# VectorE in place of GpSimd for the low parts of the weights, in the mixers and behind two norms

## The chip, the cores and the metric

The kernel runs on one NeuronCore of a Trainium2 chip. The metric is the device time of one execution in microseconds, from the chip's own clock. The engines are TensorE (PE in the profile; its weight loads are a row of their own, PEld), VectorE (DVE), ScalarE (ACT), GpSimd (POOL) and SyncE (SP), whose queue issues the loads of weights from memory. Each engine works through its own instructions in their order; semaphores order the engines among each other.

## The reference, cut to what matters

Two blocks of a language model follow each other on 256 tokens of width 1024: a first with two layers (a gated delta net and an mLSTM, each followed by a convolutional feed-forward), and a second with one layer (SwiGLU, a stage of three mixers, SwiGLU). Everything is float32. The stage that the change touches most is the mixer stage of the second block:

```python
def second_block(x, mem, ...):
    x = x + 0.5 * swiglu(rmsnorm(x, ffn1_norm), ffn1_w_gu, ffn1_w_down)
    h = rmsnorm(x, mix_norm)
    z = h @ w_in                                    # 1024 x 5280
    u = gelu(z[..., COL_U:COL_V]); v = gelu(z[..., COL_V:COL_CQ])
    y_a = spatial_gating(u, v, sg_ln_g, sg_ln_b, sg_w, sg_b)
    y_b = mla(z[..., COL_CQ:COL_CKV], z[..., COL_CKV:COL_KR], z[..., COL_KR:COL_QM], positions, ...)
    y_c = memory_attention(z[..., COL_QM:COL_GATE], mem, ...)
    gates = sigmoid(z[..., COL_GATE:] + b_gate)     # three gates of width 1024
    merged = (gates[0] * (y_a @ w_branch_a) + gates[1] * (y_b @ w_branch_b) + gates[2] * (y_c @ w_branch_c))
    x = x + merged @ w_out
    x = x + 0.5 * swiglu(rmsnorm(x, ffn2_norm), ffn2_w_gu, ffn2_w_down)

def first_block(x, ...):                            # for each of its two layers
    hs = hs + keep * rms_norm(mix, norm_w[i, 1])    # the sandwich norms: one behind the mixer,
    f = conv_ffn(rms_norm(hs, norm_w[i, 2]), ...)   # one ahead of the feed-forward
    hs = hs + keep * rms_norm(f, norm_w[i, 3])
```

## The kernel before

Activations stand with features on the partitions and tokens along the free axis, so a linear layer is a row of 128x128 weight blocks against 256 to 272 tokens. Float32 products are made of three matmuls: each operand is split into a rounded high part and a low part (what the rounding left), and TensorE adds high times high, high times low and low times high. For weights, `wload` does this block by block: SyncE loads a block of 512 KB into `wraw`, ScalarE rounds it into `wh`, and an elementwise subtraction `wl = wraw - wh` makes the low part. Three buffers of each name rotate (`p_raw` and `p_hl`, three each): a load may start when the subtraction and the rounding have read the old `wraw`, and a rounding may write `wh` when TensorE has read the old one.

Who subtracts is settled in `wload`. On VectorE it is one instruction for the whole block (128x1024); on GpSimd it is two of half the width (128x512). Blocks are counted in `nload`; `seg` counts the stages: 0 the gated delta net, 1 the first feed-forward, 2 the mLSTM, 3 the second feed-forward, 4 the first SwiGLU, 5 the mixers with their output projection, 6 the last SwiGLU. GpSimd subtracts in the delta net and the mLSTM (`ordered` is off there), everywhere in the mixers (`mixing` is on), for the first blocks after a norm in stages 1 and 3 (up to `near_load`, set from `POOL_FIRST`), and for every second or fourth block where `POOL_EVERY` says so.

Behind a sandwich norm (`mix_end`) VectorE works through a chain that is written out by hand: the residual (`mw`, `hst`), the normalized features (`xn`), ScalarE's rounding of them (`xhl`, high) and VectorE's low part of them (`xhl`, low), two of eight features at a time. TensorE starts the next linear layer feature by feature as these arrive (`linears_g`). Then come the feed-forward's evictions `fy`.

In the mixers many short chains run on VectorE beside the big products: the reciprocal square root by Newton steps (`rq_v`, `rq_a`, `rq_y`, a few columns wide), the layer norm of `v` (`sgst`, `sgv`), the rotary embedding of queries and keys (`qtok`, `ktok`, `qsq`), softmax maxima (`smx`), and the eviction `py` of a product in PSUM, whose bank TensorE needs for a later product. The order of TensorE's instructions is settled while the program is built, by a small planner (`Threads`) that keeps a clock per engine and picks the thread whose inputs are due first; it knows the work that goes through `self.V`, `self.A` and `self.G`, but not what goes straight to `nc.gpsimd`. VectorE's and ScalarE's orders come from the framework's scheduler, which has a timeline of its own.

In the profile nearly all instructions have one line, L190 (the recording helper), so groups go by tile names; subtractions sent straight to `nc.gpsimd` have line L383.

Of the kernel before, what the change touches and what calls it, by code (L numbers as in the profile page):

```python
# [78 lines left out]


NW = (0, 1, 1)
POOL_FIRST = (0, 4, 2, 2, 0, 0, 0)
POOL_EVERY = (0, 0, 0, 2, 4, 0, 4)


# [123 lines left out]
class Kern:  # L209
# [147 lines left out]
    def wload(self, w, k0, nk, c0, nc_, pieces=1, late=None, own=None, eng=None):  # L357

        key = w.tensor.name, k0, c0
        if key in self.ready:  # L360
            return self.ready.pop(key)
        tile = own or (lambda name, dt: (self.p_raw if name == "wraw" else self.p_hl).tile(
            [128, nk, nc_], dt, tag=name, name=name))
        r = tile("wraw", F32)
        self.A.ahead = self.V.ahead = self.G.ahead = True
        h, l = tile("wh", F32R), tile("wl", F32R)
        self.SY.dma_start(
            r[:], w[k0 * 128:(k0 + nk) * 128, c0:c0 + nc_].rearrange("(k p) c -> p k c", p=128))
        self.nload = getattr(self, "nload", 0) + 1
        every = POOL_EVERY[self.seg]  # L370
        if eng is not None:
            pass
        elif not self.ordered or self.mixing or self.nload <= self.near_load or every and self.nload % every == 0:
            eng, pieces = self.nc.gpsimd if self.ordered or self.mixing else self.G, 2
        else:
            eng = self.V
        sub = [(slice(k, k + nk // pieces), slice(None)) for k in range(0, nk, nk // pieces)] if nk >= pieces else [
            (slice(None), slice(c, c + nc_ // pieces)) for c in range(0, nc_, nc_ // pieces)]
        inst = self.A.copy(h[:], r[:])

        def low():
            for a, b in sub:
                eng.tensor_tensor(l[:, a, b], r[:, a, b], h[:, a, b].bitcast(F32), ALU.subtract)  # L383

        if late is None:
            low()
        else:
            if self.ordered:
                self.order(inst)
            late.append(low)  # L390
        self.A.ahead = self.V.ahead = self.G.ahead = False
        return h, l
# [315 lines left out]
    def mix_end(self, src, wcol, N, loads=(), late=1, full=True):  # L708


        late = len(loads) - late
        self.prefetch(loads[:late])
        yield self.part_done
        pm = yield from self.colsum_end(0, self.macc[1])
        pb = yield from self.colsum(self.mwacc, N, "pc1")
        yield ["pc0"]
        pa = yield from self.colsum(self.mcross, N, "pc0")
        r = self.sm(N, "rstd", "rstd")
        X = self.xslots(N)
        c = self.ssq[:, T - N:]  # L720
        r2 = self.r = self.sm(N, "rstd2", "rstd2")
        u = self.sm(N, "sqn", "y")
        w = [self.mw[k // 2][:, k % 2:k % 2 + 1, :N] for k in range(2)] + [self.mw[n][:, :, :N] for n in (1, 2, 3)]
        s2 = [self.hst[:, k:k + n, T - N:] for k, n in ((0, 1), (1, 1), (2, 2), (4, 2), (6, 2))]
        y = {}

        def residual(n):
            self.tt(w[n], w[n], r[:, None, :].to_broadcast([128, w[n].shape[1], N]), ALU.mult)
            self.tt(s2[n], s2[n], w[n], ALU.add)

        def high(*ks):
            for k in ks:
                if full:
                    y[k] = self.sm(N, "xn", "y")
                    self.stt(y[k][:], src[k], self.pv(wcol + k), r2[:], ALU.mult, ALU.mult)
                    self.A.copy(X[k][0], y[k][:])
                else:
                    self.act(X[k][0], src[k], AF.Copy, scale=self.pv(wcol + k))

        def low(*ks):  # L740
            for k in ks:
                if full:
                    self.tt(X[k][1], y[k][:], X[k][0].bitcast(F32), ALU.subtract)
                else:
                    self.last_low = self.stt(X[k][1], src[k], self.pv(wcol + k), X[k][0].bitcast(F32), ALU.mult, ALU.subtract)

        def sums():
            self.tt(u[:], pb[:], r[:], ALU.mult)
            self.stt(u[:], pa[:], 2.0, u[:], ALU.mult, ALU.add)
            self.tt(u[:], u[:], r[:], ALU.mult)  # L750
            self.tt(c, u[:], c, ALU.add)

        def token_scale():

            sums()
            self.rstd(r2[:], c, D, NW[1])
            self.near_load = self.nload + POOL_FIRST[self.seg]

        wlow = []
        with self.tc.manual_schedule(engines={mybir.EngineType.DVE, mybir.EngineType.Activation}):  # L760
            self.rstd(r[:], pm[:], D, NW[0])
            self.seg += 1
            self.near_load = 0
            if full:
                sums()
                self.rstd(r2[:], c, D, NW[1], (lambda: residual(0), lambda: residual(1)))
                high(0, 1)
                residual(2)
                low(0, 1)
                high(2, 3)  # L770
                self.prefetch(loads[late:], wlow, self.V)
                residual(3)
                low(2, 3)
                high(4, 5)
                for f in wlow:
                    f()
                residual(4)
                low(4, 5)
                high(6, 7)
                low(6, 7)  # L780
                self.near_load = self.nload + POOL_FIRST[self.seg]
            else:
                residual(0)
                high(0)
                residual(1)
                high(1)
                low(0)
                residual(2)
                high(2, 3)
                low(1)  # L790
                self.prefetch(loads[late:], wlow, self.V)
                residual(3)
                high(4, 5)
                low(2, 3)
                for f in wlow:
                    f()
                residual(4)
                high(6, 7)
                low(4, 5, 6, 7)
                self.mid = token_scale  # L800
        return X
# [1019 lines left out]
    def add_tile(self, m, ps, scale):  # L1821


        if m == 5:
            self.table("natural_log_exp_and_others")
        x = self.x2[m]
        if scale == 0.5:
            y = self.sm(S, "ady", "y")
            self.stt(y[:], ps, scale, self.r[:], ALU.mult, ALU.mult)
            self.tt(x, x, y[:], ALU.add)  # L1830
        else:
            self.stt(x, ps, scale, x, ALU.mult, ALU.add)
        h, l = self.nextX[m]
        w = self.pv(self.nextw + m)
        self.act(h, x, AF.Copy, scale=w)
        self.stt(l, x, w, h.bitcast(F32), ALU.mult, ALU.subtract)
        self.square(self.macc, m, x, S, "ma")
        if m == KD - 2:
            self.th.add([self.early([self.macc], S)])
        elif m == KD - 1:  # L1840
            self.scale_done = Event()
            self.seg += 1
            self.near_load = self.nload + POOL_FIRST[self.seg]
            self.th.add([self.token_scale(self.macc, S, self.scale_done)])

    def mem_prep(self):
# [604 lines left out]
```

## Time and profile before

| what | value |
|---|---|
| median of 3 runs | 1661.56 us (1658.22 to 1662.08) |
| the profiled execution | 1655.78 us, its span 1654.0 us |
| PE busy | 1547.4 us (94%) |
| DVE busy | 1124.6 us (68%) |
| ACT busy | 929.0 us (56%) |
| POOL busy | 581.0 us (35%) |

The profiled execution is one more run, 5.8 us under the median of the three. The span runs from its first to its last instruction; 1.8 us lie around it. A busy row counts the time in which the engine had an instruction in work, also where that instruction was held up. The granted clock is the share of full speed (1 is 2.4 GHz, 0.5 is 1.2 GHz) that TensorE had.

### The profile page before, as it was taken

How to read it: one execution, taken by the hardware profiler on the slowest of the kernel's cores; microseconds unless marked ns; L12 is line 12 of the kernel's file. 1: busy time of each engine (PE TensorE's matmuls, PEld its weight loads, DVE VectorE, ACT ScalarE, POOL GpSimd, SP SyncE). 2: the span in 40 equal slices, each digit the busy share in tenths (PEclk: the TensorE clock that was granted, in tenths of full speed). 3: DMA queues.
4: the chain of work that ended last, by engine and by line, in shares of the span. 5: the costliest groups of instructions: out<-in, count | busy, mean ns of one | idle time of the engine just before them, and what ended most of it. 6: DMA issues, size and time to landing. Idle time of an engine off the chain costs nothing.

```text
span 1654.0 us, 31168 instructions
## 1 busy us (share of the span) xinstructions
PE 1547.4 (94%) x11932; PEld 1461.7 (88%) x11932; DVE 1124.6 (68%) x2231; ACT 929.0 (56%) x1885; POOL 581.0 (35%) x535
## 2 busy tenths in 40 slices
PE   7889888899899999899899999999997899999999
PEld 5778777789799998888799999999986899999987
DVE  6788877757888857357877758665659653566643
ACT  4567667656566645445566645554554664564442
POOL 3674555320200000551143533312265548511221
PEclk9899999999999999999999999999998999999999
DMA  5331221226365553344356665665553435656664
GB/s 160 91 90 52 77 60 45 77 90 196 108 186 187 178 176 112 105 116 133 110 179 190 187 182 156 206 193 176 174 166 106 128 90 156 182 160 192 183 187 153
DMA packets 239099, 235.39 MB, mean 142 GB/s; under 512 B 11510, under 2 KB 226406, under 8 KB 238950
## 3 DMA queue, kind: packets, MB, share of 16 engines
q1 hardware_dynamic: 238326, 231.86, 46.7%
q8 instruction: 94, 1.54, 0.4%
q0 software_dynamic: 496, 1.41, 0.4%
q14 instruction: 55, 0.45, 0.1%
q10 hardware_dynamic: 128, 0.13, 0.0%
HBM read 232.32 MB, written 1.05 MB: 141 GB/s over the span
## 4 chain that ended last, share of the span: by engine, by line
PE 68%; DVE 22%; ACT 5%; DMA 3%; issue 2%; POOL 0%; SPq 0%; ACTq 0%; DVEq 0%; POOLq 0%
PE ps L190 53%; PE pst L190 4%; DVE cy L190 3%; DVE rq_a L190 3%; DVE RT L190 2%; ACT wh L190 2%; DVE wl L190 1%; DVE rq_y L190 1%; DVE xn L190 1%; PE rsp L190 1%; DVE xhl L190 1%; DMA wraw<-in_ffn_w_up_dram 1%; DVE on L190 1%; PE w L190 1%; PE up L190 1%
## 5 line engine op out<-in xcount | busy, mean ns | idle before, releaser
L190 PE MATMUL ps<-xhl,wh 128*128 128x256 f32 (+2 forms) x4496 | 859.6, 293 | 28.2 <-DVE py L190 7.4
L190 PEld LDWEIGHTS ps<-xhl,wh 128*128 128x128 f32 x4496 | 701.4, 192 | 37.9 <-DVE xhl L190 8.0
L190 ACT CAST wh<-wraw 128x1024 fp32r<-128x1024 f32 (+2 forms) x436 | 448.1, 1029 | 382.0 <-PE ps L190 255.7
L190 PE MATMUL ps<-xhl,wl 128*128 128x256 f32 (+2 forms) x2248 | 625.5, 287 | 0.0
L383 POOL TENSOR_TENSOR wl<-wraw,wh 128x512 fp32r<-128x512 f32 (+3 forms) x264 | 336.1, 1297 | 645.1 <-ACT wh L190 597.2
L190 PEld LDWEIGHTS ps<-xhl,wl 128*128 128x128 f32 x2248 | 423.6, 192 | 0.0
L190 DVE TENSOR_TENSOR wl<-wraw,wh 128x1024 fp32r<-128x1024 f32 (+2 forms) x237 | 285.7, 1206 | 166.1 <-ACT wh L190 161.5
L190 POOL TENSOR_TENSOR wl<-wraw,wh 128x512 fp32r<-128x512 f32 x134 | 174.5, 1324 | 150.9 <-ACT wh L190 134.1
L190 PE MATMUL ps<-hh,wh 128*128 128x256 f32 (+1 forms) x1056 | 191.1, 283 | 0.0
L190 PEld LDWEIGHTS ps<-hh,wh 128*128 128x128 f32 x1056 | 163.2, 189 | 0.0
L190 PE MATMUL ps<-hh,wl 128*128 128x256 f32 (+1 forms) x528 | 149.8, 284 | 0.0
L190 DVE SCALAR_TENSOR_TENSOR fy<-ps,pvt,fy 128x256 f32<-128x256 f32 (+2 forms) x176 | 84.9, 488 | 25.7 <-ACT fy L190 23.8
L190 PEld LDWEIGHTS ps<-hh,wl 128*128 128x128 f32 x528 | 99.4, 188 | 0.2 <-DVE wl L190 0.2
L190 DVE SCALAR_TENSOR_TENSOR cy<-cx,pvt,cy 128x271 f32<-128x271 f32 (+2 forms) x96 | 74.4, 778 | 13.7 <-ACT cy L190 12.7
L190 DVE TENSOR_TENSOR hh<-fy,hh 128x256 fp32r<-128x256 f32 (+1 forms) x88 | 66.3, 755 | 14.0 <-ACT hh L190 13.9
L190 POOL MEMSET mvt<- 128x4 f32 x4 | 0.4, 102 | 176.1 <-PE ps L190 176.1
L190 DVE TENSOR_TENSOR py<-ps,rstd 128x256 f32<-128x256 f32 x72 | 30.1, 421 | 38.0 <-PE ps L190 38.0
L190 ACT ACTIVATE fy<-ps,pvt 128x272 f32<-128x272 f32 (+1 forms) x88 | 49.6, 568 | 10.8 <-PE ps L190 10.2
L190 PE MATMUL pst<-wh,hh 128*128 128x512 f32 x176 | 55.1, 394 | 0.0
L190 ACT CAST hh<-fy 128x256 fp32r<-128x256 f32 (+1 forms) x88 | 35.7, 407 | 29.0 <-DVE fy L190 28.4
L190 PE MATMUL ps<-og,wh 128*128 128x272 f32 x256 | 49.5, 291 | 0.1
L190 DVE CAST_PREDICATED RT<-lvl,w 128x512 f16<-128x512 uint8 x67 | 44.9, 684 | 6.7 <-PE w L190 6.3
(521 smaller groups left out, 2400.6 us busy)
## 6 DMA issues: line engine op xcount, KB each, us to landing
wraw<-in_ffn_w_up_dram SPq DMA_DIRECT2D x88, 512.0 KB
wraw<-in_ffn_w_gu_dram SPq DMA_DIRECT2D x88, 512.0 KB
wraw<-in_ffn_w_down_dram SPq DMA_DIRECT2D x79, 512.0 KB
wraw<-in_gdn_w_in_dram SPq DMA_DIRECT2D x48, 512.0 KB
wraw<-in_w_in_dram SPq DMA_DIRECT2D x41, 512.0 KB
wraw<-in_ml_w_in_dram SPq DMA_DIRECT2D x24, 512.0 KB
wraw<-in_gdn_w_out_dram SPq DMA_DIRECT2D x16, 512.0 KB
wraw<-in_mem_w_kv_dram SPq DMA_DIRECT2D x8, 512.0 KB
```

The costliest lines, as they stand in the source:

```text
L190: r = f(*args, **kw)
L383: eng.tensor_tensor(l[:, a, b], r[:, a, b], h[:, a, b].bitcast(F32), ALU.subtract)
```

## The change

VectorE makes all low parts of weights in the mixers (stage 5). Behind the sandwich norms a table `QUIET` says for how many blocks GpSimd stays out, in place of a table that says for how many it is put in: three blocks in stages 1 and 3 (in stage 1 GpSimd has no later turn either). In stage 3 GpSimd's turn at every second block begins after these three. All else in `wload` stays.

```diff
-POOL_FIRST = (0, 4, 2, 2, 0, 0, 0)
+QUIET = (0, 3, 0, 3, 0, 0, 0)
 POOL_EVERY = (0, 0, 0, 2, 4, 0, 4)
...
         if eng is not None:
             pass
-        elif not self.ordered or self.mixing or self.nload <= self.near_load or every and self.nload % every == 0:
-            eng, pieces = self.nc.gpsimd if self.ordered or self.mixing else self.G, 2
+        elif not self.ordered or self.nload > self.near_load and every and self.nload % every == 0:
+            eng, pieces = self.nc.gpsimd if self.ordered else self.G, 2
         else:
             eng = self.V
...
-                self.near_load = self.nload + POOL_FIRST[self.seg]
+                self.near_load = self.nload + QUIET[self.seg]
```

GpSimd's list loses 8 half subtractions in the first feed-forward, 6 in the second and 120 in the mixers (110 of them 128x512, the rest of smaller blocks): 4, 3 and 60 blocks. VectorE gains as many whole subtractions. SyncE's list is the same.

On VectorE, behind the first norm (stage 1), the four blocks come in between the last two pairs of features and among the evictions of the feed-forward:

```order
 L190 TENSOR_TENSOR hst<-hst,mw 128x544
 L190 TENSOR_TENSOR xhl<-xn,xhl 128x272 x2
+L190 TENSOR_TENSOR wl<-wraw,wh 128x1024
 L190 SCALAR_TENSOR_TENSOR xn<-hst,pvt,rstd_6112 128x272 x2
+L190 TENSOR_TENSOR wl<-wraw,wh 128x1024
 L190 TENSOR_TENSOR xhl<-xn,xhl 128x272 x2
 L190 SCALAR_TENSOR_TENSOR fy<-ps,pvt,fy 128x271 x2
 L190 SCALAR_TENSOR_TENSOR fy<-ps,pvt,fy 128x270 x2
+L190 TENSOR_TENSOR wl<-wraw,wh 128x1024
```

Two subtractions now stand inside the chain of the features, one ahead of `xn` and one ahead of the last `xhl`; behind the norm of stage 3 it is the same pattern.

On VectorE in the mixers, from the middle of the two layer norms (`sgv` is scaled by `sglg`, then shifted by `sglb`) to the evictions `py` of the first products of `u`:

```order
+L190 TENSOR_TENSOR wl<-wraw,wh 128x1024
 L190 TENSOR_TENSOR sgv<-sgv,sglg 128x512
-L190 SCALAR_TENSOR_TENSOR rq_a<-rq_y 128x4
-L190 SCALAR_TENSOR_TENSOR rq_y<-rq_a,rq_y 128x4
+L190 TENSOR_TENSOR py<-ps,rstd 128x256
+L190 SCALAR_TENSOR_TENSOR rq_a<-rq_y 128x4
+L190 SCALAR_TENSOR_TENSOR rq_a<-rq_y 128x1
+L190 SCALAR_TENSOR_TENSOR rq_y<-rq_a,rq_y 128x4
+L190 TENSOR_TENSOR py<-ps,rstd 128x256
 L190 TENSOR_TENSOR sgv<-sgv,sglb 128x512
```

The subtraction shown is the fifth since the first `sgst`; the first `py` stands ahead of the three wide operations of the second layer norm, behind which it stood before. Four more subtractions follow up to the first finished `qtok`.

On TensorE at the same place, between the products of `u` (`ps`, the last two rows of them) and the transposes of the queries (`qktp`):

```order
 L190 MATMUL ps<-xhl,wh 128x256 x2
 L190 MATMUL ps<-xhl,wl 128x256
+L190 MATMUL pst<-wh,xhl 128x512 x2
+L190 MATMUL pst<-wl,xhl 128x512
+L190 MATMUL pst<-wh,xhl 128x512 x2
+L190 MATMUL pst<-wl,xhl 128x512
...
 L190 MATMUL qktp<-eye,qtok 96x128 x4
```

Six such groups of three matmuls (the projection of the memory queries) are moved from behind the transposes to ahead of them.

## Rows read from the trace of the kernel before

**Rows 1.** The page's costliest groups: name, count, busy us, mean ns, idle before.

```profile
L383 POOL TENSOR_TENSOR wl<-wraw,wh 128x512 fp32r<-128x512 f32 (+3 forms) x264 | 336.1, 1297 | 645.1 <-ACT wh L190 597.2
L190 DVE TENSOR_TENSOR wl<-wraw,wh 128x1024 fp32r<-128x1024 f32 (+2 forms) x237 | 285.7, 1206 | 166.1 <-ACT wh L190 161.5
```

**Rows 2.** Timeline of VectorE behind the first norm: start us, us, what.

```profile
435.69 0.79 DVE L190 TENSOR_TENSOR xhl<-xn,xhl 128x272 fp32r<-128x272 f32 x2
436.39 0.91 DVE L190 SCALAR_TENSOR_TENSOR xn<-hst,pvt,rstd 128x272 f32<-128x272 f32 x2
...
439.75 2.94 DVE L190 TENSOR_TENSOR xhl<-xn,xhl 128x272 fp32r<-128x272 f32 x2
442.61 2.93 DVE L190 SCALAR_TENSOR_TENSOR xn<-hst,pvt,rstd 128x272 f32<-128x272 f32 x2
445.47 1.01 DVE L190 TENSOR_TENSOR xhl<-xn,xhl 128x272 fp32r<-128x272 f32 x2
```

**Rows 3.** Timeline of GpSimd, behind the first norm and in the mixers.

```profile
439.51 5.74 POOL L383 TENSOR_TENSOR wl<-wraw,wh 128x512 fp32r<-128x512 f32 x4 [82.24 <-ACT wh L190]
...
1239.26 12.52 POOL L383 TENSOR_TENSOR wl<-wraw,wh 128x512 fp32r<-128x512 f32 x10 [2.18 <-ACT wh L190]
```

**Rows 4.** Windows: us, busy of PE, PEld, DVE, ACT, POOL (instructions), clock, DMA share, GB/s.

```profile
439.00:449.00 10.00, 6.57 (x28) 5.57 (x28) 7.69 (x9) 3.15 (x7) 5.74 (x4) 0.66 0.51 157
815.00:825.00 10.00, 7.22 (x34) 6.42 (x35) 7.80 (x10) 3.30 (x7) 5.32 (x5) 0.66 0.51 151
...
1237.88:1257.58 19.70, 13.38 (x92) 12.61 (x90) 19.49 (x46) 8.85 (x14) 12.52 (x10) 0.91 0.60 174
1250.00:1276.00 26.00, 16.36 (x95) 13.28 (x94) 25.97 (x93) 7.71 (x15) 10.15 (x9) 0.80 0.35 101
1300.00:1350.00 50.00, 43.09 (x327) 40.05 (x327) 39.58 (x138) 28.75 (x74) 23.03 (x18) 0.97 0.37 110
...
1360.00:1400.00 40.00, 40.00 (x339) 39.71 (x339) 15.72 (x37) 20.43 (x34) 30.13 (x24) 1.00 0.52 147
```

**Rows 5.** Groups of VectorE from 1239.35 to 1251.8 us, columns as in rows 1.

```profile
L190 DVE TENSOR_TENSOR rq_a<-rq_a,rq_v 128x1 f32<-128x1 f32 x4 | 5.0, 1257 | 0.0
L190 DVE SCALAR_TENSOR_TENSOR rq_y<-rq_a,rq_y 128x1 f32<-128x1 f32 x4 | 3.8, 974 | 0.0
L190 DVE SCALAR_TENSOR_TENSOR rq_a<-rq_y 128x1 f32<-128x1 f32 x4 | 3.3, 857 | 0.0
```

**Rows 6.** Timeline of VectorE in the mixers, from the first layer norm to `py`.

```profile
1237.88 0.70 DVE L190 BATCH_NORM_STATS2 sgst<-sgv 128x6 f32<-128x512 f32 x1 [1.34 <-ACT sgv L190]
...
1239.20 0.16 DVE L190 SCALAR_TENSOR_TENSOR rq_a<-rq_y 128x1 f32<-128x1 f32 x1
...
1257.58 0.42 DVE L190 TENSOR_TENSOR py<-ps,rstd 128x256 f32<-128x256 f32 x1
```

**Rows 7.** Timeline of TensorE: the two longest waits in the mixers, in brackets.

```profile
1258.06 0.80 PE L190 MATMUL ps<-xhl,wh 128*128 128x256 f32 x2 [6.79 <-DVE py L190]
...
1266.37 0.64 PE L190 MATMUL qktp<-eye,qtok 128*96 128x128 f32 x4 [2.52 <-DVE qtok L190]
```

**Rows 8.** Groups of VectorE from 1257.6 to 1266.3 us, ahead of the first transposes.

```profile
L190 DVE TENSOR_TENSOR qsq<-qtok,rcos 128x64 f32<-128x64 f32 x3 | 1.7, 576 | 0.0
L190 DVE SCALAR_TENSOR_TENSOR rq_y<-rq_a,rq_y 128x4 f32<-128x4 f32 x4 | 1.7, 430 | 0.0
L190 DVE TENSOR_TENSOR qsq<-qtok,rsin 128x64 f32<-128x64 f32 x2 | 1.5, 753 | 0.0
```

**Rows 9.** Groups of VectorE from 1300 to 1338.2 us, the three costliest of 25.

```profile
L190 DVE TENSOR_TENSOR rq_a<-rq_a,rq_v 128x4 f32<-128x4 f32 x15 | 4.3, 299 | 0.1
L190 DVE SCALAR_TENSOR_TENSOR rq_a<-rq_y 128x4 f32<-128x4 f32 x15 | 4.3, 293 | 0.1
L190 DVE SCALAR_TENSOR_TENSOR rq_y<-rq_a,rq_y 128x4 f32<-128x4 f32 x15 | 3.8, 261 | 0.1
```

**Rows 10.** Waits of VectorE: us in total, times, the longest.

```profile
DVE wl L190 <- ACT wh L190: 161.5, 144, 4.4
```

More of the change, by code (lines that the diff above doesn't have):

```diff
@@ L780, in mix_end @@
                 low(6, 7)
-                self.near_load = self.nload + POOL_FIRST[self.seg]
+                self.near_load = self.nload + QUIET[self.seg]
             else:
@@ L1842, in add_tile @@
             self.seg += 1
-            self.near_load = self.nload + POOL_FIRST[self.seg]
+            self.near_load = self.nload + QUIET[self.seg]
             self.th.add([self.token_scale(self.macc, S, self.scale_done)])
```

## The prediction

> **What bounds the kernel now.** I read the page's busy rows first: TensorE works 94% of the span, so only what lets it wait, or what lowers its clock, can move the time much. The windows come next, to find where it waits. From 1360 to 1400 us it is busy for all 40.00 us at clock 1.00 while GpSimd subtracts for 30.13 us [rows 4]: in the second half of the mixers nothing is to be had. The waits lie in four places that the change touches: the ten microseconds behind the first norm (TensorE busy 6.57, clock 0.66), the like place behind the third (7.22, 0.66), the mixers from 1250 to 1276 us (16.36 of 26.00, clock 0.80) and from 1300 to 1350 us (43.09 of 50.00, clock 0.97) [rows 4].
>
> Then the timeline of VectorE at these places, which is the view that matters here. Behind the first norm a pair of low parts `xhl` takes 0.79 us and a pair `xn` 0.91 us; three microseconds later the same instructions take 2.94 and 2.93 us [rows 2]. What differs is GpSimd: its four half subtractions run from 439.51 to 445.25 us [rows 3]. In the mixers a Newton step one column wide takes 0.16 us at 1239.20 [rows 6], and from 1239.35 to 1251.8 us twelve such steps take 12.1 us, most of them 1.2 [rows 5], while ten half subtractions run back to back on GpSimd for 12.52 us, 1.25 us each [rows 3]. So a VectorE instruction that meets a running subtraction of GpSimd stands still until that half is over, and the next one meets the next half. "VectorE busy 19.49 of 19.70 us" in that window [rows 4] is therefore mostly standing. TensorE pays for it: it waits 6.79 us for `py`, and then 2.52 us for `qtok` [rows 7].
>
> **The change part by part: the two norms.** Taken away: the standing. Added: subtractions of 1.21 us each on VectorE [rows 1], two of them inside the chain of the features, at both places. Before, the chain from the low parts of features 4 and 5 to those of 6 and 7 runs from 439.75 to 446.48 us, 6.73 us [rows 2]. After: 0.79 + 1.21 + 0.91 + 1.21 + 0.79 = 4.91 us. That is 1.8 us, and TensorE waits feature by feature for this chain, so it gets them. The window behind the third norm shows the same picture (VectorE 7.80 busy, GpSimd 5.32) [rows 4], so I take 1.8 us there too: **-3.6 us**. From below: if ScalarE's rounding of `wh` is late for the inserted subtractions, they hold the chain by their mean wait of 1.1 us (161.5 us over 144 waits [rows 10]) and the gain is lost. From above: the clock of 0.66 over ten microseconds costs 3.4 us at each place [rows 4]; if the shorter waits kept it at 1, that came on top. I do not count it, since most of TensorE's pauses ahead of the drop come from the norm itself and stay. The other two blocks of the first feed-forward and the third of the second lie among the evictions; they bring VectorE 1.21 us each and free it of two halves that it met there. I put that at nothing: TensorE is fed from three buffers there, and if this cover were gone it would cost those 1.21 us each, 3.6 us.
>
> **The mixers from 1237.88 us.** From the first `sgst` to `py` VectorE needs 19.70 us without a pause [rows 4, 6]. Of this the twelve steps give back 12.1 - 12 x 0.16 = 10.2 us [rows 5, 6]. Five subtractions come in: 5 x 1.21 = 6.05 us. Two smaller ones stand just ahead, where VectorE idled for 1.34 us [rows 6]. Three operations 512 wide move behind `py`; half as wide as a subtraction, an estimated 0.6 us each, 1.8 in all. So `py` comes 19.70 - 10.2 + 6.05 - 1.8 = 13.75 us after 1237.88, at 1251.6 us in place of 1257.58. TensorE began to wait at 1258.06 - 6.79 = 1251.27 us, so some 0.8 us of this wait are left.
>
> What is late next is `qtok` for the first transposes. From `py` to there VectorE needs 8.7 us now (1257.58 to 1266.3). Four steps `rq_y` of 430 ns give back 0.27 each; five products `qsq` 64 wide, which I put at 0.22 us undisturbed (between 0.16 for one column and 0.42 for 256 [rows 6]), give back 3 x 0.36 + 2 x 0.53: 3.2 us in all [rows 8]. Four subtractions (4.8), the three wide operations from above (1.8) and two more `py` (0.8) come in: 12.9 us, so `qtok` is ready at 1264.5 us, 1.8 us earlier than now. TensorE has by then also done six groups of three matmuls that it did afterwards: 18 x 512 columns at 2.4 GHz, 3.8 us. That makes 5.6 us. Of the low clock (0.80 over 26.00 us is 5.2 us [rows 4], much of it while TensorE waits anyway) I add 1.4 us: **-7 us** for this place. Bounds: if the moved matmuls only fill a wait that is then needed elsewhere, 1.8 us are left; the whole wait and the whole clock are 9.6 + 5.2 = 14.8 us.
>
> This is the place where a rule speaks against the change. The Trainium skill, "Perfetto Trace Analysis", section "Optimizing Scalar/DVE Operations", says that where VectorE is saturated it may make sense to move work off it, even to GpSimd, though the two share a port and it may not help. By its first half the sum here would be nine subtractions more on a full engine, 10.9 us later and not 7 earlier. The rows side with its second half: the engine is full of standing, not of work [rows 4, 5].
>
> **The mixers from 1300 us, and the rest.** Up to 1338 us VectorE is nearly full again. Seven subtractions come in, 8.5 us. The three costliest forms, 45 steps at 299, 293 and 261 ns in place of 160, give back 5.6 us [rows 9], and the other 22 forms some more. So VectorE has about as much to do as before, in shorter pieces that wait for nobody: **-1 us**, between +2.9 (those three forms alone give back) and -6.9 (TensorE's whole wait there [rows 4]). The other 44 or so blocks of the mixers cost nothing: up to 1236 us, and from 1360 us on, where VectorE was busy 15.72 of 40.00 us [rows 4] and gets some 12 blocks, 14.6 us; without this cover each would cost 1.21 us. Loads move by no place in SyncE's queue; a block's `wraw` is free after one subtraction of 1.21 us and not two of 1.30 [rows 1].
>
> **Sum:** -3.6 - 7 - 1 = -11.6 us. The profiled execution took 1655.78 us (span 1654.0 and 1.8 around it), so 1644.2 us; the median of the runs is 5.8 us higher, and I set the same difference against it: 1661.56 - 11.6 = **1650 us**.
>
> **The rivals.**
>
> *The wait moves into VectorE's queue (slower).* A subtraction on GpSimd could wait for ScalarE's `wh` without holding anyone; on VectorE the Newton steps, `py` and the evictions stand behind it. For: VectorE's own subtractions waited 144 times for 1.1 us on average, up to 4.4 [rows 10]. Against: those waits lie mostly in stages where VectorE had nothing else to do. Sixteen subtractions stand in the two full stretches of the mixers. If each waits 0.7 us, the 11.6 us are gone; at 1.1 us it is +6 us, at 1.5 us +12 us: about 1670 us.
>
> *VectorE was really full (slower).* If the stretched instructions had another cause than GpSimd, nothing comes back, and the nine and seven subtractions of the two stretches and the four in the norms' chains are all added: 20 x 1.21 = 24 us, 1686 us. This is the rule above as a mechanism of this kernel. Against it: the same form of instruction is short or long according to GpSimd alone [rows 2, 3, 5, 6].
>
> *The gain is hidden (no change).* Behind `py` and `qtok` stand others: a load, a rounding, the next attention step. If TensorE gets only the norms' 3.6 us and the mixers end where they ended, 1658 us. For: the mixers are many short chains that take turns at being last, and the window from 1300 us waits without any single long wait.
>
> *The clock comes back too (more).* If TensorE's waits become short enough that it is granted full speed throughout, add 2 x 3.4 us at the norms and most of the wait and clock in the mixers: -3.6 - 6.8 - 12 - 4 = -26 us, 1635 us.
>
> **How the numbers follow.** What a measurement of this kernel tells from no change is about 0.3%, 5 us. My case (7 to 17 us less) 0.50, the clock's case 0.20, a small gain of 5 to 7 us 0.06: faster 0.76. Hidden, or gain and new waits even: 0.16. The two slower cases together 0.08. My case alone spans 1644 to 1655 us. The range reaches down nearly to the clock's case and up into the hidden one, 1638 to 1660 us; it leaves out the slower cases and the far end of the clock's.
>
> **What would show it.** Right: behind both norms `xhl` and `xn` pairs keep to 0.8 and 0.9 us, with subtractions of 1.2 us between them; in the mixers no Newton step of 1.2 us is left; TensorE's wait for `py` falls below 1.5 us, and its wait at `qktp` stays near 3; the span from the last SwiGLU on is unchanged. Wrong: subtractions on VectorE that idle for `wh` inside the two full stretches; steps still stretched with GpSimd silent; TensorE waiting as long for other releasers; or a clock of 1.00 behind the norms, which would make the gain larger.

## The result and the profile after

The changed kernel takes 1635.8 us (median of four runs, 1634.5 to 1638.6), the kernel before 1660.2 us on the same chip: a ratio of 0.986 [0.984, 0.988], 24 us less. The forecast was 1650 us, with a range down to 1638: the sign was right, but the gain is twice as large. The profiled execution took 1638.56 us (span 1636.7, mean granted clock 0.980).

The page's groups of subtractions, as in [rows 1] (name, count, busy us, mean ns, idle before):

```profile
L190 DVE TENSOR_TENSOR wl<-wraw,wh 128x1024 fp32r<-128x1024 f32 (+3 forms) x304 | 365.4, 1202 | 198.0 <-ACT wh L190 193.4
L383 POOL TENSOR_TENSOR wl<-wraw,wh 128x512 fp32r<-128x512 f32 (+2 forms) x130 | 165.7, 1296 | 700.4 <-ACT wh L190 676.0
```

VectorE has 67 subtractions more, 80 us of work, but is busy for only 17 us more (1141.3 us in place of 1124.6). Behind the first norm its timeline, as in [rows 2], reads now:

```profile
439.58 0.79 DVE L190 TENSOR_TENSOR xhl<-xn,xhl 128x272 fp32r<-128x272 f32 x2
440.29 1.22 DVE L190 TENSOR_TENSOR wl<-wraw,wh 128x1024 fp32r<-128x1024 f32 x1
441.42 0.90 DVE L190 SCALAR_TENSOR_TENSOR xn<-hst,pvt,rstd 128x272 f32<-128x272 f32 x2
442.25 1.22 DVE L190 TENSOR_TENSOR wl<-wraw,wh 128x1024 fp32r<-128x1024 f32 x1
443.38 0.78 DVE L190 TENSOR_TENSOR xhl<-xn,xhl 128x272 fp32r<-128x272 f32 x2
```

No pair is stretched any more. In the mixers a Newton step takes 0.15 us, and the first `py` comes 11.96 us after the first layer norm, in place of 19.70 [rows 6]:

```profile
1235.70 0.70 DVE L190 BATCH_NORM_STATS2 sgst<-sgv 128x6 f32<-128x512 f32 x1 [1.45 <-ACT sgv L190]
...
1238.15 0.15 DVE L190 SCALAR_TENSOR_TENSOR rq_a<-rq_y 128x1 f32<-128x1 f32 x1
...
1247.66 0.42 DVE L190 TENSOR_TENSOR py<-ps,rstd 128x256 f32<-128x256 f32 x1
```

Windows at the places of [rows 4], moved with the program (us, busy of PE, PEld, DVE, ACT, POOL, clock, DMA share, GB/s):

```profile
439.00:449.00 10.00, 7.17 (x40) 6.74 (x41) 7.74 (x14) 5.09 (x8) 0.00 (x0) 0.83 0.50 157
812.00:822.00 10.00, 7.81 (x62) 7.39 (x61) 7.75 (x14) 6.61 (x10) 0.00 (x0) 1.00 0.54 159
1235.70:1247.66 11.96, 11.96 (x81) 11.36 (x80) 11.68 (x41) 8.87 (x14) 0.00 (x0) 1.00 0.71 211
1245.00:1271.00 26.00, 22.89 (x137) 19.28 (x136) 23.56 (x90) 10.01 (x17) 0.00 (x0) 0.87 0.46 130
1290.00:1340.00 50.00, 48.37 (x394) 46.25 (x393) 39.72 (x156) 34.01 (x86) 0.00 (x0) 1.00 0.41 116
```

Over longer windows around the two norms (425 to 470 and 795 to 845 us in both kernels) the clock rose from 0.92 to 0.96 and from 0.93 to 0.97. The second window above reads 1.00 only because the stretch in which TensorE is granted 1.2 GHz, the lower of its two levels, lies ahead of it now, at about 806 to 809 us.

From 1290 to 1340 us TensorE is busy for 48.4 of 50 us, where it was 43.1. What it still waits for in the mixers (1195 to 1440 us; us in total, times, longest):

```profile
PE qktp L190 <- DVE qtok L190: 3.1, 1, 3.1
PE latp L190 <- DVE lacc L190: 2.5, 1, 2.5
PE ptp L190 <- ACT pexp L190: 1.3, 2, 0.8
```

The wait for `py` [rows 7] is gone, that for `qtok` is as long as it was forecast, and one for `lacc` is new.

For the stages I take the starts of TensorE's first `krp`, `qktp` and `scp`, its last `qktp` and the first `rsp` of the last norm from the timeline. Durations in us; "before 2" and "before 3" are two more profiles of the kernel before, "after 2" one more of the changed kernel (all told at the end of the experiments):

| kernel | start to `krp` | to `qktp` | to `scp` | to the last `qktp` | to `rsp` | span |
|---|---|---|---|---|---|---|
| before | 1205.2 | 61.1 | 32.9 | 46.6 | 116.5 | 1654.0 |
| before 2 | 1203.4 | 63.2 | 38.7 | 46.0 | 116.5 | 1659.5 |
| before 3 | 1205.8 | 60.6 | 38.0 | 47.9 | 116.5 | 1660.5 |
| after | 1200.3 | 60.5 | 29.4 | 39.7 | 115.2 | 1636.7 |
| after 2 | 1199.0 | 62.4 | 28.3 | 39.7 | 115.2 | 1636.3 |
| mixers only | 1201.5 | 62.0 | 35.9 | 39.7 | 115.2 | 1646.0 |
| norms only | 1200.5 | 63.1 | 39.0 | 45.6 | 116.5 | 1656.9 |
| VectorE, old order | 1199.1 | 59.0 | 33.1 | 40.2 | 115.2 | 1638.3 |
| GpSimd, new order | 1199.5 | 67.5 | 29.7 | 47.6 | 115.8 | 1652.3 |
| reads added | 1201.8 | 69.7 | 37.3 | 48.5 | 123.9 | 1672.7 |
| writes added | 1199.2 | 57.9 | 28.3 | 40.6 | 115.2 | 1632.9 |
| late on GpSimd | 1197.8 | 60.5 | 28.3 | 46.1 | 115.8 | 1640.2 |
| early on GpSimd | 1198.0 | 64.9 | 32.6 | 43.2 | 115.2 | 1645.6 |

Rest: the last SwiGLU, 187.5 us and the tail in every one of them. What the first column's kernels share scatters by 2 to 3 us from run to run (the delta net alone by that much), so small differences there say nothing.

### The profile page after: what moved, and what is told of

It reads as the page before. It is cut to its first block, busy times and chain, and to the rows that moved or that the text cites. A ratio compares the mean times of both kernels' runs of the same rounds, so it can differ in the third digit from the quotient of the medians.

```text
span 1636.7 us, 31051 instructions
## 1 busy us (share of the span) xinstructions
PE 1544.8 (94%) x11932; PEld 1460.3 (89%) x11932; DVE 1141.3 (70%) x2298; ACT 928.6 (57%) x1885; POOL 411.2 (25%) x401
## 4 chain that ended last, share of the span: by engine, by line
PE 73%; DVE 17%; ACT 5%; DMA 2%; issue 2%; SPq 0%; POOL 0%; ACTq 0%; DVEq 0%; POOLq 0%
PE ps L190 56%; PE pst L190 6%; DVE cy L190 3%; ACT wh L190 2%; DVE rq_a L190 2%; DVE wl L190 2%; DVE RT L190 2%; PE rsp L190 1%; PE up L190 1%; PE warm L190 1%; PE w L190 1%; PE memp L190 1%; DVE rq_y L190 1%; DMA wraw<-in_ffn_w_up_dram 1%; DVE on L190 1%
## 5 line engine op out<-in xcount | busy, mean ns | idle before, releaser
L190 DVE TENSOR_TENSOR wl<-wraw,wh 128x1024 fp32r<-128x1024 f32 (+3 forms) x304 | 365.4, 1202 | 198.0 <-ACT wh L190 193.4
L383 POOL TENSOR_TENSOR wl<-wraw,wh 128x512 fp32r<-128x512 f32 (+2 forms) x130 | 165.7, 1296 | 700.4 <-ACT wh L190 676.0
L190 DVE TENSOR_TENSOR fy<-ps,sg 128x256 f32<-128x256 f32 x44 | 18.2, 417 | 41.4 <-PE ps L190 38.3
```

Source lines behind the costliest of these rows:

```text
L190: r = f(*args, **kw)
```

## The experiments

All start from the changed kernel, and all ratios are to the kernel before on the same chip.

**Mixers or norms.** Each half of the change alone: the old table with its condition, and the old mixers with the new table.

```diff
 # mixers only (and the table POOL_FIRST again)
-        elif not self.ordered or self.nload > self.near_load and every and self.nload % every == 0:
+        elif not self.ordered or self.nload <= self.near_load or every and self.nload % every == 0:
 # norms only
-        elif not self.ordered or self.nload > self.near_load and every and self.nload % every == 0:
+        elif not self.ordered or self.mixing or self.nload > self.near_load and every and self.nload % every == 0:
...
```

> The mixers' part of the change alone; behind the norms GpSimd subtracts as before. Two theories of where the change's 1.4% (24 us) comes from. Standing: VectorE no longer stands still while a half subtraction of GpSimd runs; then the parts add up, and by the two traces (TensorE comes out of the first norm 1.3 us earlier, of the third 2.9 us, of the mixers another 12.3 us) this kernel keeps all but 4 us: ratio to before 0.987 to 0.990. Order: TensorE's new order in the mixers, which follows from the planner knowing of the subtractions, brings it; this kernel has that order too, so it cannot tell the two apart, but must come out at the same 0.987 to 0.990. A ratio above 0.994 would mean that the norms carry more than their place in the trace shows.

> The norms' part alone; GpSimd subtracts in the mixers as before, and TensorE's order is that of before. My prediction had 3.6 us for the two norms, the traces show 4.2 us: ratio 0.997 to 0.998. If the waits behind the norms were only moved (they are taken up again by the next full stretch of VectorE), 1.000. If keeping the clock up matters more than the waits themselves, 0.995 or less.

Measured: 0.993 [0.991, 0.996] and 0.999 [0.998, 1.000]. Both gained less than was expected, and the second's interval reaches to no gain at all. Together that is 13 us of 24 by the ratios: the parts do not add up. The table says where: the mixers alone have the whole gain from the first `scp` on (39.7 us), but lose 6.5 us ahead of it (35.9 in place of 29.4). That stretch comes back below.

**VectorE's standing or TensorE's order.** The change also moves matmuls ahead, since the planner sees the subtraction now. First VectorE subtracts behind the planner's back (TensorE's order as before); then GpSimd subtracts in the mixers and the planner is told that VectorE does (TensorE's order as changed).

```diff
 # VectorE, old order                       # GpSimd, new order
+        elif self.mixing:                  +        elif self.mixing:
+            eng = self.nc.vector           +            eng, pieces, plan = self.nc.gpsimd, 2, True
...
+            if plan:
+                self.th.note("V", [l[:]], [r[:], h[:]], nk * nc_, True)
```

> As the changed kernel, but in the mixers the subtractions go to VectorE past the planner, so TensorE's order is that of before. Standing: nearly the whole gain stays, since VectorE's full stretches are relieved just the same: ratio to before 0.986 to 0.990. The moved matmuls (six groups, 3.8 us of work ahead of the transposes) are what it can lose. Order: without the new order most of the mixers' gain is gone and only the norms' 4 us and little more are left: 0.995 to 0.998.

> The converse: norms as in the changed kernel, in the mixers GpSimd subtracts as before, but the planner is told that VectorE does it, so TensorE's order is that of the changed kernel. Standing: VectorE still meets the halves, so no more than the norms' 4 us and a little for the matmuls moved ahead into a wait (up to 4 us): 0.995 to 0.998. Order: the mixers' gain comes with the order: 0.987 to 0.990.

Measured: 0.989 [0.987, 0.991] and 0.998 [0.996, 1.000], as the standing has it. By the traces TensorE's order is that of the kernel before in the first and that of the changed kernel in the second, so the new order is worth little by itself.

**What of GpSimd makes VectorE stand.** VectorE keeps its subtractions, and GpSimd gets something to do behind each of them: in one kernel it subtracts the halves of `wh` from themselves into the raw tile, which is dead by then; in the other it fills that tile with zeros.

```diff
+            if self.mixing and nk > 1:
+                for k in (0, nk // 2):                                    # reads added
+                    x = h[:, k:k + nk // 2, :].bitcast(F32)
+                    self.nc.gpsimd.tensor_tensor(r[:, k:k + nk // 2, :], x, x, ALU.subtract)
...
+                for k in (0, nk // 2, 0, nk // 2):                        # writes added
+                    self.nc.gpsimd.memset(r[:, k:k + nk // 2, :], 0.0)
```

> The changed kernel, in which GpSimd, behind each of VectorE's subtractions in the mixers, subtracts the two halves of `wh` from themselves and writes the zeros over the weight's raw tile, which nobody reads any more. The output stays what it was. If VectorE stands still for GpSimd's reading, the gain of the mixers is lost and VectorE has its new subtractions on top: ratio to the kernel before 1.000 to 1.020, first mixers' projection to the start of the last feed-forward 255 to 275 us (before 257.1, changed kernel 244.8), Newton steps of 1.2 us again. If the gain came from something else in taking the subtractions off GpSimd (a shorter way from load to matmul, an earlier free buffer), it stays: 0.984 to 0.990.

> The same place and the same four matmul operand blocks, but GpSimd fills the raw tile with zeros four times (four halves) instead of subtracting: it is as busy, it writes, and it reads nothing. If only GpSimd's reading makes VectorE stand, the gain stays: ratio 0.983 to 0.991, mixers 243 to 249 us, Newton steps of 0.16 us. If any work on GpSimd that touches the memory makes it stand, it is like the run with the reads: 1.000 to 1.020.

Measured: 1.010 [1.008, 1.012] with the reads, 0.986 [0.984, 0.988] with the writes. With reads, the stretch from the first `krp` to the first `rsp` took 279.3 us, more than the 275 expected at most. GpSimd's groups of the mixers, VectorE's from 1237 to 1300 us, TensorE's longest wait, and ScalarE's wait for loads of `w_in` from 1195 to 1485 us (us, times, longest):

```profile
L387 POOL TENSOR_TENSOR wraw<-wh 128x512 f32<-128x512 f32 x110 | 135.9, 1261 | 98.8 <-DVE wl L190 61.8 <-DVE rq_a L190 26.1 <-DVE smx L190 5.3
...
L190 DVE SCALAR_TENSOR_TENSOR rq_a<-rq_y 128x4 f32<-128x4 f32 x12 | 5.1, 429 | 0.0
L190 DVE SCALAR_TENSOR_TENSOR rq_y<-rq_a,rq_y 128x4 f32<-128x4 f32 x12 | 3.8, 319 | 0.0
L190 DVE TENSOR_REDUCE qss<-qsq 128x4 f32<-128x384 f32 x4 | 2.2, 540 | 0.0
...
PE qktp L190 <- DVE ktok L190: 7.1, 1, 7.1
...
ACT wh L190 <- DMA wraw<-in_w_in_dram: 32.6, 17, 5.8
```

The same with writes, with one more of VectorE's groups (from 1200 to 1485 us; its mean is 0.17 us in the changed kernel):

```profile
L386 POOL MEMSET wraw<- 128x512 f32 x220 | 106.4, 528 | 97.8 <-DVE wl L190 97.4 <-DVE rq_v L190 0.2
...
L190 DVE SCALAR_TENSOR_TENSOR rq_a<-rq_y 128x4 f32<-128x4 f32 x21 | 3.6, 173 | 0.1
L190 DVE TENSOR_REDUCE qss<-qsq 128x4 f32<-128x384 f32 x6 | 3.3, 548 | 0.0
L190 DVE SCALAR_TENSOR_TENSOR rq_y<-rq_a,rq_y 128x4 f32<-128x4 f32 x21 | 3.2, 157 | 0.1
...
L190 DVE TENSOR_SCALAR rq_v<-qss 128x4 f32<-128x4 f32 x8 | 2.4, 298 | 0.1
...
ACT wh L190 <- DMA wraw<-in_w_in_dram: 16.3, 13, 2.7
```

106 us of writes cost nothing; the kernel with 136 us of reads is 39 us longer (1676.8 against 1637.8). With reads the means of the steps are 429 and 319 ns, with writes 173 and 157. The reduction, which reads one tile, takes 0.54 us in either. For all of VectorE's instructions from 1195 to 1485 us I add up what each takes above the median of its form in the changed kernel. An estimate of the standing comes out: some 51 us in the first profile of the kernel before, 4 in the changed kernel, 52 with reads, 9 with writes. So the reads bring the old standing back, on top of VectorE's own subtractions.

The 39 us are not all standing. With reads GpSimd also holds the raw tiles longer (loads waited 133 us for it in this window, 108 with writes), and ScalarE waited 32.6 us for loads; the two are not parted. In the kernel before ScalarE's wait was 4.3 us, so late loads are not what made that one slow. The fills too hold each raw tile some 2 us longer (four of 528 ns), and the gain stays: it does not come from buffers that are free earlier.

The Trainium skill, "SBUF — State Buffer", section "Who interferes with whom", says that a VectorE instruction with two inputs in SBUF contends with a GpSimd instruction that reads SBUF, not with one that only writes it, and that whoever loses blocks for the whole instruction. These two runs agree on reads against writes, and steps of 1.2 us beside halves of 1.25 [rows 3, 5] agree on the blocking. The agreement is not complete: beside the fills some TENSOR_SCALAR instructions, which have one input, still stretch to the end of a fill, as `rq_v<-qss` above (0.30 us in the mean, 0.57 at most), and a few steps that stand in line right behind such a one stretch with it (0.50 at most).

**Which stretch gives what.** The mixers' blocks (counted in `nmix`) from the 30th on (from about 1291 us), or those up to the 29th, go back to GpSimd, with the planner told as above.

```diff
+        elif self.mixing and self.nmix > 29:     # late; early: self.nmix <= 29
+            eng, pieces, plan = self.nc.gpsimd, 2, True
```

> The changed kernel with the subtractions of the mixers' blocks from the 30th on (those from about 1291 us) back on GpSimd, TensorE's order as in the changed kernel. If each stretch makes its own gain, the 7 us from 1300 us on and the 1 us at the end are lost: ratio 0.989 to 0.993, first `scp` to the last `qktp` 45 to 48 us (39.7 in the changed kernel). If the later stretch gained only because the earlier one ended sooner, nothing is lost: 0.984 to 0.988.

> The mirror image: the first 29 blocks of the mixers on GpSimd, the later ones on VectorE, TensorE's order as in the changed kernel. If each stretch makes its own gain, only the 4 us up to the first `scp` are lost: ratio 0.987 to 0.990, first `krp` to first `scp` 92 to 96 us (94.0 before, 89.9 changed), first `scp` to the last `qktp` 39 to 42 us. If the later gain hangs on the earlier one: 0.993 to 0.997.

Measured: 0.989 [0.988, 0.991] and 0.993 [0.991, 0.995]. The first came out as "each stretch makes its own gain" has it: from `scp` to the last `qktp` it takes 46.1 us, as before the change. The second lost more than I gave it, and lies at the edge of the other theory's range. Its trace says where: the early stretch is longer than I had thought (97.6 us from `krp` to `scp`, 89.9 in the changed kernel), and the later one loses half of its gain too (43.2 us). GpSimd's last five halves (5.66 us) still fall into that later stretch, so this run does not part the two cleanly.

**Why parts do not add: one place in VectorE's order.** Four kernels in which VectorE also makes the mLSTM's low parts (`not self.seg` added to `not self.ordered`). In three of them one block of the mixers, the 23rd or the 22nd, gets another engine:

```diff
-        elif not self.ordered or self.nload > self.near_load and every and self.nload % every == 0:
+        elif not self.ordered and not self.seg or self.nload > self.near_load and every and self.nload % every == 0:
...
+        elif self.mixing and self.nmix == 23:    # or 22; or nc.scalar.copy(l, r) in low()
+            eng, pieces, plan = self.nc.gpsimd, 2, True
```

> The changed kernel, in which VectorE also makes the low parts of the 21 blocks of the mLSTM (637 to 800 us), GpSimd no more. In its trace VectorE's instructions stand there for some 20 us above their undisturbed durations, and TensorE waits some 14 us in all, mostly for VectorE. If standing is the price, as in the mixers, TensorE gets back 3 to 6 us: ratio to the kernel before 0.981 to 0.984 (the changed kernel has 0.986). If the gain of the mixers was theirs alone (TensorE waits in the mLSTM for chains that do not meet the subtractions), no change: 0.985 to 0.987.

> The run with the mLSTM on VectorE, in which one single block of the mixers, the 23rd, is subtracted by GpSimd; on VectorE nothing else changes its place. This is the subtraction that stood there ahead of the rotations of `ktok` at 1271 us, where TensorE then waited 3.1 us at `qktp` and the stretch from the first `sgy` to the first `scp` took 29.9 us in place of the changed kernel's 23.8. If that one place in VectorE's order cost the 6 us, the wait falls below 1.5 us, the stretch takes 24 to 26 us and the ratio to the kernel before is 0.983 to 0.986. If the stretch is long for another reason (the clock ahead of it, a load), it stays at 29 to 31 us and the ratio at 0.987 to 0.990.

> The run with the mLSTM on VectorE, in which ScalarE copies the raw tile of the mixers' 23rd block in place of its low part (it leaves that one low part out of the result; the copy takes some 1.05 us on ScalarE, which is idle there). VectorE keeps its order, with nothing ahead of the rotations of `ktok` and no GpSimd beside them. Worked out from the two runs before: the rotation pair ends 1.1 us earlier than with VectorE's subtraction and 2.15 us earlier than beside GpSimd's, so TensorE's wait for `ktok` is 2.0 us by both (3.1 - 1.1, 4.1 - 2.15). If the wait is what makes the stretch from the first `sgy` to the first `scp` long, it takes 24 to 28.5 us; if something else does, 29 to 32 us.

> The same with the 22nd block on GpSimd in place of the 23rd. On VectorE the scheduler then sets the 23rd block's subtraction behind the pair of rotations and the `sgyy` behind `ktok`, as in the changed kernel. If that order is what keeps TensorE from waiting there, the wait for `ktok` is below 1.5 us, the stretch from the first `sgy` to the first `scp` takes 23.5 to 26 us and the ratio is 0.982 to 0.987, although one block more stands on GpSimd; otherwise 29 to 32 us and 0.988 to 0.992.

Measured, with the stretch from the first `sgy` to the first `scp` (23.8 us at clock 0.99 in the changed kernel):

| kernel | ratio | `sgy` to `scp` | clock in it | TensorE's wait for `ktok` |
|---|---|---|---|---|
| mLSTM on VectorE | 0.989 [0.986, 0.991] | 29.9 | 0.89 | 3.1 |
| and block 23 on GpSimd | 0.991 [0.989, 0.993] | 32.2 | 0.84 | 4.1 |
| and block 23 copied by ScalarE | 0.986 [0.984, 0.989] | 28.8 | 0.88 | 2.0 |
| and block 22 on GpSimd | 0.986 [0.984, 0.988] | 24.2 | 1.00 | 0.3 |

The first missed both of its expectations: the mLSTM got some 2 us shorter, which is within the scatter, and the mixers, where nothing was edited, 6.7 us longer; there the scheduler had put a subtraction ahead of the rotations of `ktok` on VectorE (first pair of lines below). The second did not put that right and missed both of its own. GpSimd's two halves now stood over the pair of rotations itself, which takes 0.35 us alone; VectorE's timeline:

```profile
1267.07 2.50 DVE L190 TENSOR_TENSOR ktok<-qsq 128x64 f32<-128x64 f32 x2
```

In this stretch one block on GpSimd at the wrong moment cost more than the same block on VectorE (32.2 against 29.9 us; the ratios overlap). The third took both away, and the wait fell to the 2.0 us worked out from the other two, with its releaser now named as ScalarE's copy; the stretch stayed at 28.8 us, between its two expectations. So the subtraction alone is not it. In the fourth VectorE's order there is like the changed kernel's (the first two products of `ktok` ahead of `sgyy`, the pair of rotations ahead of the subtraction), although a block more is on GpSimd; its wait is 0.3 us, its stretch 24.2. The pair and the subtraction in the first of the four, and then in the fourth:

```profile
1271.17 1.22 DVE L190 TENSOR_TENSOR wl<-wraw,wh 128x1024 fp32r<-128x1024 f32 x1
1272.30 0.35 DVE L190 TENSOR_TENSOR ktok<-qsq 128x64 f32<-128x64 f32 x2
...
1272.69 0.35 DVE L190 TENSOR_TENSOR ktok<-qsq 128x64 f32<-128x64 f32 x2
...
1273.84 1.23 DVE L190 TENSOR_TENSOR wl<-wraw,wh 128x1024 fp32r<-128x1024 f32 x1
```

The fourth also has one subtraction less on VectorE ahead of this place, so by itself it does not part the order from the work. The changed kernel does: with TensorE's order in the mixers the same in all five, it has that subtraction on VectorE, an order like the fourth's, no such wait and 23.8 us. The two lengths of the stretch go with the clock: 0.84 to 0.89 where the wait is 2.0 to 4.1 us, 1.00 where it is 0.3. All of this is read from the traces; the ratios of the last two kernels are equal.

**No GpSimd at all.** VectorE makes all low parts of the mLSTM and the delta net (`not self.ordered` taken out of the condition), then those of the feed-forwards too (`POOL_EVERY` all zero).

> As the run before, and in the delta net at the start (20 to 360 us) VectorE makes the low parts too, 46 blocks. Standing sums to some 70 us there, the subtractions to 46 x 1.21 = 56 us; TensorE waits some 40 us in that stage, and its order is planned anew, since the planner counts the subtraction on another engine. By the standing theory VectorE has 14 us less to do: the delta net gets 2 to 8 us shorter, ratio 0.977 to 0.983. If here VectorE's queue is the price (it is over 0.8 busy from 100 to 300 us, and its products wait behind subtractions that wait for `wh`), it gets longer: 0.990 to 1.010.

> No subtraction on GpSimd anywhere in the kernel: the run before, and the feed-forwards' every second or fourth block on VectorE too. TensorE is busy 199 of 200 us from 1000 to 1200 us with GpSimd subtracting in part of it, so nothing is to be had there; from 800 to 1000 us it is busy 193.5, with 62 halves on GpSimd. By the standing theory equal to the run before or up to 3 us shorter; if VectorE is full there without them, 2 to 6 us longer than the run before.

Measured: 0.991 [0.988, 0.993] and 0.989 [0.986, 0.992]. The delta net gets some 4 to 7 us longer (its norm's first `rsp` starts at 363.5 and 362.6 us, at 358.1 and 356.5 in the two profiles of the changed kernel), which fits the first run's second expectation, that VectorE's queue is the price; I cannot part that from TensorE's newly planned order. The second run's median is 6 us under the first's, which neither of its expectations had; the intervals overlap. None of these beats the changed kernel.

**The kernels unchanged, profiled again.** The pair of profiles differs by 17 us, the medians by 24.

> The kernel before, unchanged, profiled once more. Its first profile took 1655.78 us, 4.4 us under the median of its runs, and the pair of profiles differs by 17.2 us where the medians differ by 24.4. If the first profile was a lucky run of before, this one takes 1657 to 1663 us, and its stages show where the 2 to 7 us come from: in the mixers (first `krp` to the last feed-forward 257.1 us in the first profile) if their waits and half clock scatter, or in the delta net and the feed-forwards if loads do.

> The same a third time, so that a stage that is longer once can be told from one that is longer as a rule: 1657 to 1663 us.

> The changed kernel, unchanged, profiled once more: 1634 to 1639 us, mixers 243 to 246 us (244.8 in its first profile), since TensorE's waits there are short and few. If its mixers scatter by more than 3 us, they have two states in the changed kernel too.

Profiled at 1661.3, 1662.3 and 1638.1 us. By the table the changed kernel repeats itself, and the kernel before has 38 us from `qktp` to `scp` in two of three profiles and 32.9 in the first alone. The kernel with the norms alone, whose mixers are those of before, has 39.0. Here is what happened in the second profile, on GpSimd, VectorE and TensorE, and the window from `sgy` to `scp`:

```profile
1274.60 2.48 POOL L383 TENSOR_TENSOR wl<-wraw,wh 128x512 fp32r<-128x512 f32 x2 [2.81 <-ACT wh L190]
...
1274.63 1.31 DVE L190 TENSOR_TENSOR qsq<-ktok,rcos 128x64 f32<-128x64 f32 x1
1275.87 1.30 DVE L190 TENSOR_TENSOR qsq<-ktok,rsin 128x64 f32<-128x64 f32 x1
...
1277.36 0.74 DVE L190 TENSOR_TENSOR sgyy<-sgy,sgu 128x256 f32<-128x256 f32 x2
...
1278.25 0.77 PE L190 MATMUL sgy<-sgb,sgsel 128*128 128x128 f32 x2 [4.01 <-DVE sgyy L190]
...
1269.16:1305.29 36.13, 32.12 (x179) 25.77 (x178) 18.35 (x62) 16.83 (x44) 17.59 (x16) 0.86 0.29 78
```

And the same in the first profile:

```profile
1275.88 4.41 POOL L383 TENSOR_TENSOR wl<-wraw,wh 128x512 fp32r<-128x512 f32 x2 [4.32 <-ACT wh L190]
...
1274.41 0.22 DVE L190 TENSOR_TENSOR qsq<-ktok,rcos 128x64 f32<-128x64 f32 x1
1274.55 0.22 DVE L190 TENSOR_TENSOR qsq<-ktok,rsin 128x64 f32<-128x64 f32 x1
...
1274.96 0.75 DVE L190 TENSOR_TENSOR sgyy<-sgy,sgu 128x256 f32<-128x256 f32 x2
...
1275.85 0.46 PE L190 MATMUL sgy<-sgb,sgsel 128*128 128x128 f32 x2 [0.34 <-DVE sgyy L190]
...
1269.92:1299.22 29.30, 28.96 (x179) 23.67 (x177) 15.49 (x59) 15.85 (x40) 18.63 (x16) 0.98 0.35 96
```

In the second profile GpSimd's two halves begin just as the products `qsq` do, and these take 1.3 us each in place of 0.22. `sgyy` comes 2.4 us later, TensorE waits 4.0 us, and its next matmuls take 0.77 us in place of 0.46: it is granted the lower of its two levels (1.2 and 2.4 GHz) for a while, and the window's mean is 0.86; the third profile has the same wait (4.0) and 0.90. In the first GpSimd waited 1.5 us longer for ScalarE's `wh`, and its halves began behind the `qsq`. That execution was one of the shorter ones of this kernel, and all my sums stood on it.

## Why the prediction was off

Against the two usual profiles of before (means, and the mean of the two after) the stages give: up to `krp` -4.9 us, to `qktp` -0.5, to `scp` -9.5, to the last `qktp` -7.2, to `rsp` -1.3; in all -23.4 of the medians' -24.4 us.

- *The norms, -3.6.* Right by the traces. The chain from features 4 and 5 to 6 and 7 takes 4.58 us (4.91 forecast, 6.73 before). From the norm to the end of the feed-forward the first got 1.4 us shorter and the second 2.4: -3.8. The chains got 2.2 and 1.7 us shorter, so the better clock behind them (0.92 to 0.96, 0.93 to 0.97), which I had not counted, left no trace in the sum. The times show less: the norms alone are 2.6 us under the kernel before (medians), and the interval reaches to nothing.
- *The mixers from the first layer norm, -7.* Right in its steps: no Newton step of 1.2 us is left, `py` comes after 11.96 us (13.75 forecast), its wait is 0 (0.8), that for `qtok` 3.1 (about 3). The 6.8 us of the old wait went to the matmuls moved ahead (3.8), to a wait of 2.5 us for `lacc`, and to 0.6 more at `qtok`, so up to `qktp` nothing is gained; the moved matmuls are paid out behind it. The new wait is the first rival in small: `lacc` stood behind a subtraction that itself had waited 1.48 us for ScalarE's `wh`. Up to the first `scp` the first pair of profiles gives 4.1 us, the usual ones 10; the 6 between them are the race of the `qsq`, which the prediction did not see. So it is luck that -7 lies between the two.
- *The mixers from 1300 us, -1.* This term failed. It held that VectorE would have "about as much to do as before". From the first `scp` to the last `qktp` the windows of before and after are:

```profile
1299.22:1345.86 46.64, 40.34 (x308) 37.77 (x307) 39.00 (x135) 27.12 (x66) 22.51 (x18) 0.96 0.36 105
1290.19:1329.87 39.68, 38.05 (x308) 36.27 (x307) 34.48 (x140) 26.19 (x63) 0.00 (x0) 1.00 0.42 119
```

With eight subtractions (9.8 us) on it, VectorE is busy for 4.5 us less: the rest of its work gave back some 14 us (three short instructions fewer lie in the second window). I had priced the standing of the three costliest forms [rows 9], 5.6 us, and let "the other 22 forms some more" make up the rest of 8.5; in fact these stood at least as long as the three: by the durations of each form here and in the changed kernel, 6.4 us against 5.8. The largest of them, before and after:

```profile
L190 DVE TENSOR_TENSOR qtok<-qsq 128x64 f32<-128x64 f32 x4 | 2.5, 663 | 0.0
L190 DVE TENSOR_TENSOR qtok<-qsq 128x64 f32<-128x64 f32 x4 | 0.7, 209 | 0.0
```

TensorE's waits in these windows fell from 6.3 to 1.6 us, where I had let it keep nearly all of them. The term measured -7.2, just beyond its lower bound of -6.9; the run with the late blocks on GpSimd puts this stretch at 46.1 against 39.7 us.
- *The sum against the profiled execution.* This failed too. I moved the difference from one profiled run to the median "the same", and noted that it was 5.8 us under it, without asking which stage those 5.8 us were in. They lay between `qktp` and `scp`, in the mixers: there the usual run of before stands for `qsq`, and the change takes that away as well.
- *The rivals.* The wait did not move into VectorE's queue: in the two full stretches (1235.7 to 1261 and 1290 to 1328 us) its subtractions waited for `wh` four times, 2.2 us in all. VectorE was not full: its 0.99 busy was mostly standing, which the reads on GpSimd brought back. The gain was not hidden. The clock's case named the right time (1635) with partly the wrong reason: the clock is at 1.00 from 1290 us on, but only part of the way up at the norms and at 0.87 from 1245 to 1271 us, where TensorE still waits for `qtok`. What holds of it: with the clock that falls behind them, waits of 3.1 and 4.0 us cost 6 to 7 (29.9 against 23.8 us, 36.1 against 29.3).

What stays open is why exactly VectorE's order in one stretch follows from edits elsewhere (the scheduler's choice), how much of the longer delta net is its own new order, and how much of the 39 us with reads is standing and how much late loads.

## What to carry to other kernels

A busy share does not tell work from standing: compare the same instruction with and without the other engine running, and sum that over all forms, not the costliest. When the profiled run lies well off the median, find the stage that differs before a sum is made against it. And where GpSimd only has to write, let it; work with which it reads belongs where VectorE has no chain that TensorE waits for.

## What the hardware showed

That 106 us of fills on GpSimd made VectorE stand only some 6 us more and cost the kernel nothing, while 136 us of reads made it stand some 48 us more, in a kernel 39 us longer. And one race of 1.5 us between GpSimd and VectorE went with 5 to 6 us of one stage and of the whole profile, as 4.0 us of wait and the matmuls at half clock behind it (0.77 us in place of 0.46).
